# Attention and output projection: slots of one head become slots of two heads, with the parts of both heads issued kind by kind

## Chip, cores and metric

The kernel runs on one core of a Trainium2 chip. The metric is device time in microseconds of one execution, the lower the better. An execution profiled by the hardware gives the trace from which all rows below come. PE is TensorE's matmul stream, PEld its weight loads, DVE is VectorE, ACT is ScalarE, POOL is GpSimd, SP the queue that issues most transfers.

## The reference, cut to what matters

One encoder layer over two sequences of 1024 and 2048 tokens (24 blocks of 128 tokens), width 1024. After RMSNorm and one input projection, half of the width goes through a bidirectional state space model with a gated linear unit, the other half through windowed attention; both halves are normed, gated, concatenated and projected.

```python
def _attn_branch(q, k, v, sink, rel_bias):   # 8 heads of 64, 2 KV heads, blocks of 128 queries
    ...                                      # kw, vw: the block before, the block itself, the block after
    scores = jnp.einsum('bnqkgd,bnskd->bnkgqs', qb, kw)
    scores = scores * (HEAD_DIM ** -0.5) + bias
    scores = jnp.where(valid, scores, NEG_INF)            # |rel| <= 128
    m = jnp.maximum(jnp.max(scores, axis=-1, keepdims=True), sink_l)
    p = jnp.exp(scores - m)
    denom = jnp.sum(p, axis=-1, keepdims=True) + jnp.exp(sink_l - m)
    out = jnp.einsum('bnkgqs,bnskd->bnqkgd', p / denom, vw)
...
mixed = jnp.concatenate([_rmsnorm(y_ssm, ssm_norm_w) * jax.nn.silu(z_ssm),
                         _rmsnorm(y_attn, attn_norm_w) * jax.nn.silu(z_attn)], axis=-1)
return x + mixed @ w_out                                  # then a final RMSNorm
```

## The kernel before

The first part of the program (projection, state space model, gated linear unit) ends at about 896 us of the span and is not touched. What follows is the attention with the output projection: one software pipeline over the 24 blocks. A period p has eight slots h = 0 to 7, one per head, and in period p five blocks are at work: block p (scores), p-1 (transposes of the probabilities, first value product), p-2 (second value product, norm, gate), p-3 (output projection) and p-4 (final norm, store). Each engine runs its instructions strictly in the order in which the Python code issues them, so the order of calls in `attn_slot` is the order of work on PE, ACT, DVE and POOL; waits between engines come from the tiles, which are pools of a few buffers. All matrices are fp32 split into a high and a low part.

What a slot of one head issues, with the names that stand in the rows:

- `a_qk` (L1361, L1365): two matmuls into a score buffer `pssc` (two buffers, tag "sc"), then one DVE operation that adds the bias into `s` and takes the row maximum.
- `b_tr` (L1404 to L1417): two or three PE transposes of `s` into `pt` (two buffers), an ACT copy to `ph` (and `hs`, odd heads), and DVE subtractions to `pl` (and `hs`).
- `a_exp` (L1379): the exponential on ACT.
- `c_mm` (L242 to L244): two steps of the output projection, six matmuls with 512 columns into `pn`.
- once in a period: `b_pv(block p-2, second KV head)` at h = 0 and `b_pv(block p-1, first KV head)` at h = 4 (L1429): ten matmuls into `pv`, then an ACT copy (L1432) and a DVE sum (L1433) to `vlo`. The first needs `ph`, `pl` and `hs` of heads 4 to 7 of its block. `b_out` (L1442): four transposes of `vlo` into `tm`, at h = 1 and h = 5. `b_fin` at h = 2, `b_gate` (L1461, DVE) and `c_fin2` (L1527, DVE) at h = 5. `c_mix` (L1498 to L1500) at h = 6: four transposes of the gated block into `pm`, an ACT copy to `mh` and a DVE subtraction to `ml`. `c_gate` (L1482) and the second half of `c_ssm` (L1490) are POOL operations on 128x512.

The value products and the transposes of `c_mix` use the same single buffer of PSUM, by their tag:

```python
pv = pps.tile([P, 4, P], F32, tag="pv", name="pv", bufs=1)     # b_pv
pm = pps.tile([P, 4, P], F32, tag="pv", name="pm5", bufs=1)    # c_mix
```

so the next of them can start only when DVE has read the one before (L1433 or L1500). The loop advances a clock by `tick()` once per slot; stores and a few deferred steps hang on that clock.

Of the kernel before, what the change touches and what calls it, by code (L numbers as in the profile page):

```python
# [25 lines left out]
NH = 8  # L26
# [12 lines left out]
NBLK = NTOK // P  # L39
# [7 lines left out]
def f32(t):  # L47
    return t.bitcast(F32)
# [40 lines left out]
def hymba_layer_kernel(ctx, tc, x, xt, w_in, nw, lre, lim, lstep, bre, bim, cre, cim, dsk, w_glu, bglu,  # L89
# [14 lines left out]
    def load(dst, src):  # L104
        nc.sync.dma_start(out=dst, in_=src)
# [3 lines left out]
    def store(dst, src):  # L109
        store_eng[0].dma_start(out=dst, in_=src)  # L110
# [15 lines left out]
    def tick():  # L126
        now[0] += 1
        for e in [e for e in late if e[1] <= now[0]]:
            late.remove(e)
            store(e[2], e[3])  # L130
# [11 lines left out]
    def run_soon():  # L142
        for e in [e for e in soon if e[0] <= now[0]]:
            soon.remove(e)
            e[1]()
# [760 lines left out]
    for c in range(NCH):  # L906
        for ft in range(8):
# [9 lines left out]
            if c + 1 < NCH:  # L917
# [4 lines left out]
                elif ft in (1, 2) and c:  # L922
                    i = 4 * ft - 4
# [350 lines left out]
    for s in SEQS:  # L1274
        n = s // P
# [69 lines left out]
    def wo_load(k):  # L1345
        load(wor[k % 2], w_out[k * P:(k + 1) * P])

    def wo_split(k, n):
        f = slice(n * 512, (n + 1) * 512)
        split_w(*(t[:, k - 4, f] for t in wo[1]), wor[k % 2][:, f], wsc[:, k:k + 1])  # L1350
        if n and k + 2 < KM:
            wo_load(k + 2)

    pps = ctx.enter_context(pool("ps5", space=PSUM))
    def a_qk(i, h):
        d = st[i]
        pr, hf = divmod(h, 2)
        c0, nk, ko, ne, po, bo = (d["hv"][hf][k] for k in ("c0", "nk", "ko", "ne", "po", "bo"))
        ps = pps.tile([P, 384], F32, tag="sc", name="pssc", bufs=2)
        for hl in range(2):  # L1360
            TE.matmul(ps[:, 0:ne], lhsT=d["qt"][:, hf, pr * P:(pr + 1) * P],  # L1361
                      rhs=d["kt"][:, h // 4, hl, ko:ko + ne], start=hl == 0, stop=hl == 1)
        if hf == 0:
            d["sc"][pr] = p4.tile([P, 2, 320], F32, tag="s", name="s", bufs=6)
        V.tensor_tensor_reduce(out=d["sc"][pr][:, hf, c0:c0 + nk], in0=ps[:, po:po + nk], in1=bias[:, pr, bo:bo + nk],  # L1365
                               op0=ALU.add, op1=ALU.max, scale=1.0, scalar=NEG, accum_out=d["mx"][:, h:h + 1])
# [26 lines left out]
    def b_tr(i, h):  # L1393
        d = st[i]
        kv, pp, hf = h // 4, h // 2 % 2, h % 2
        v, s_ = d["hv"][hf], d["sc"][h // 2]
        if h % 4 == 0:
            for nm in ("ph", "pl"):
                d[nm, kv] = p4.tile([P, 2, 2, 2, P], F32R, tag=nm, name=nm, bufs=2)
            d["hs", kv] = p4.tile([P, 2, 2, P], F32R, tag="hs", name="hs", bufs=2)  # L1400
        pt = pps.tile([P, 3, P], F32, tag="pt", name="pt", bufs=2)
        n = len(v["full"])
        for j, (c, _) in enumerate(v["full"]):
            TE.transpose(pt[:, j], s_[:, hf, c:c + P], ident)  # L1404
        parts = [e for e in range(2) if d["hv"][e]["part"]] if hf else []
        if parts:
            m = 64 * len(parts)
            c = 256 + 64 * parts[0]
            TE.transpose(pt[0:m, 2], s_.rearrange("p f k -> p (f k)")[:, c:c + m], ident)
        hs = [(d["hs", kv][:, e, pp], pt[64 * k:64 * k + 64, 2]) for k, e in enumerate(parts)]  # L1410
        for t, p in hs:
            A.copy(out=t[0:64], in_=p)
        ph, pl = (d[nm, kv][:, hf, 0:n, pp] for nm in ("ph", "pl"))
        A.copy(out=ph, in_=pt[:, 0:n])  # L1414
        V.tensor_tensor(out=pl, in0=pt[:, 0:n], in1=f32(ph), op=ALU.subtract)  # L1415
        for t, p in hs:
            V.tensor_tensor(out=t[64:128], in0=p, in1=f32(t[0:64]), op=ALU.subtract)  # L1417
# [18 lines left out]
    def b_out(i, kv):  # L1436
        d = st[i]
        if kv == 0:
            d["tm"] = pps.tile([P, 512], F32, tag="tm", name="tm", bufs=1)
        for h in range(4):  # L1440
            hh = 4 * kv + h
            TE.transpose(d["tm"][:, hh * HD:(hh + 1) * HD], d["ot"][:, h], ident[0:64, 0:64])  # L1442
# [21 lines left out]
    def c_load(i):  # L1464
        d = st[i]
        un, bu = divmod(d["bg"], 8)
        yt = p4.tile([P, 4, P], F32, tag="ys4", name="ys4", bufs=2)
        load(yt, yssc[un][:, bu * P:(bu + 1) * P].rearrange("(k p) t -> p k t", p=P))
        zs = p4.tile([P, 4, P], F32, tag="zs4", name="zs4", bufs=2)
        load(zs, zssc[un][:, bu * P:(bu + 1) * P].rearrange("(k p) t -> p k t", p=P))  # L1470
        za = p4.tile([P, HALF], F32, tag="za", name="za", bufs=2)
        load(za, zasc[d["bg"] * P:(d["bg"] + 1) * P])
        d.update(za=za, yt=yt, zs=zs)

    def c_load_x(i):
        d = st[i]
        d["x"] = p4.tile([P, DM], F32, tag="x4", name="x4", bufs=2)
        load(d["x"], x[d["bg"] * P:(d["bg"] + 1) * P])

    def c_gate(i):  # L1480
        d = st[i]
        G.tensor_tensor(out=d["yt"], in0=d["yt"], in1=d["zs"], op=ALU.mult)  # L1482

    def c_ssm(i):
        d = st[i]
        yt = d["yt"]
        mh = p4.tile([P, 8, P], F32R, tag="mh", name="mh", bufs=2)
        ml = p4.tile([P, 8, P], F32R, tag="ml", name="ml", bufs=2)
        A.copy(out=mh[:, 0:4], in_=yt)
        G.tensor_tensor(out=ml[:, 0:4], in0=yt, in1=f32(mh[:, 0:4]), op=ALU.subtract)  # L1490
        d.update(mh=mh, ml=ml)
# [10 lines left out]
    def c_mm(i, n, k, c0=0, c1=512):  # L1502
        d = st[i]
        if k == 0 and c0 == 0:
            d["pn", n] = pps.tile([P, 512], F32, tag="pn", name="pn", bufs=2)
        f = slice(n * 512 + c0, n * 512 + c1)
        wh, wl = (t[:, k % 4, f] for t in wo[k // 4])
        mm3(d["pn", n][:, c0:c1], d["mh"][:, k], d["ml"][:, k], wh, wl, k == 0, k == KM - 1)
# [47 lines left out]
    def ok(i):  # L1556
        return 0 <= i < NBLK

    def attn_slot(p, h):
        ia, ib, it, ic, io = p, p - 1, p - 2, p - 3, p - 4  # L1560
        if ok(ia):
            a_qk(ia, h)
        if ok(it) and h == 0:
            b_pv(it, 1)
            if it:
                c_gate(it)
        if p == 0:
            if h == 5:
                c_load(0)
        elif p == 1:  # L1570
            if h == 2:
                c_gate(0)
            elif h == 5:
                c_ssm(0)
        if ok(ib):
            b_tr(ib, h)
        if h >= 4 and ok(ia):
            a_exp(ia, h - 4)
        if h < 4 and ok(ib):
            a_exp(ib, h + 4)  # L1580
        if h == 0 and ok(ic):
            c_load_x(ic)
        if p == 2:
            c_mm(0, h // 4, h % 4)
        if ic == 0:
            c_mm(ic, h // 4, 4 + h % 4)
        elif ic == NBLK - 1 and h >= 4:
            for j in range(4):
                c_mm(ic, 1, h % 2 * 4 + j, h // 6 * 256, h // 6 * 256 + 256)
        elif ok(ic):  # L1590
            for j in range(2):
                c_mm(ic, h // 4, (h % 4) * 2 + j)
        if ic == NBLK - 1:
            c_last(ic, h)
        if h == 0 and ok(io) and io < NBLK - 1:
            c_res(io, 1)
        if h == 4 and ok(ic) and ic < NBLK - 1:
            c_res(ic, 0)
        if h == 0 and ok(ib):
            a_den(ib, 0)  # L1600
        if h == 4 and ok(ib):
            a_den(ib, 1)
            b_pv(ib, 0)
        if h == 1:
            if ok(it):
                b_out(it, 1)
            if ok(io) and io < NBLK - 1:
                c_fin1(io)
        if h == 2 and ok(it):
            b_fin(it)  # L1610
            if it:
                c_ssm(it)
        if h == 3 and ok(ia):
            a_nm(ia, 0)
        if h == (4 if p else 0) and ok(ia + 1):
            a_load(ia + 1)
        if h == 5:
            if ok(ib):
                b_out(ib, 0)
            if ok(it):  # L1620
                b_gate(it)
            if ok(io) and io < NBLK - 1:
                c_fin2(io)
        if h == 6:
            if ok(it):
                c_mix(it)
            if ok(ib) and ib:
                c_load(ib)
        if h == 7 and ok(ia):
            a_nm(ia, 1)  # L1630

    wo_load(4)
    wo_load(5)
    for p in range(NBLK + 3):
        for h in range(NH):
            tick()
            attn_slot(p, h)
            run_soon()
            if p == 1:
                wo_split(4 + h // 2, h % 2)  # L1640
    flush()


# [44 lines left out]
```

## Time and profile before

| | us |
|---|---|
| median of 3 runs | 1406.27 (1405.92 to 1414.81) |
| profiled execution, its device time | 1414.28 |
| profiled execution, span from first to last instruction | 1412.5 |
| PE busy in the span | 1336.2 (95%) |
| DVE busy | 1045.4 (74%) |
| ACT busy | 745.8 (53%) |
| POOL busy | 295.0 (21%) |

The profiled execution is 8.0 us longer than the median of the three runs and within 0.6 us of the longest of them. Its device time is 1.8 us over its span. Matmuls overlap each other and their ends are modelled, so the cost of a matmul is read as the distance from its start to the start of the next one, not as its length.

### The profile page before, as it was taken

The page shows a single profiled execution, that of the slowest core. Times are in us where ns is not written, and L with a number is a line of the kernel's source. Part 1 is how long each engine was busy: PE and PEld are TensorE (multiplying, and loading weights), DVE is VectorE, ACT ScalarE, POOL GpSimd, SP SyncE. Part 2 cuts the span into 40 slices and gives each one's busy share as a digit, 9 for nine tenths or more (in the row PEclk, how much of TensorE's full clock was granted, in tenths as well). Part 3 has the DMA queues.
Part 4 walks back from the last instruction along what each step waited for, and adds up shares of the span by engine and source line. Part 5 has one row for each costly group of instructions (what it writes and reads, how often), then busy time and mean ns, then how long its engine had stood idle before and what let it go on. Part 6 is the DMA issues. An engine that isn't in the chain of part 4 may idle for free.

```text
span 1412.5 us, 24562 instructions
## 1 busy us (share of the span) xinstructions
PE 1336.2 (95%) x8578; PEld 1190.6 (84%) x8578; DVE 1045.4 (74%) x2423; ACT 745.8 (53%) x1662; POOL 295.0 (21%) x798
## 2 busy tenths in 40 slices
PE   7998999999999998999999889879999999999997
PEld 7998999999988997887797767667888888888876
DVE  5499666344897796588588378668888888888885
ACT  6222432243345525746747567566766666666662
POOL 1143231010000000000000043513444334433442
PEclk9998999999999998999999989789999999999999
DMA  7534474655556465424424564792668866766533
GB/s 255 171 122 166 169 221 148 186 168 189 172 177 200 154 195 171 156 83 154 163 90 153 173 182 151 209 215 80 145 166 195 194 173 156 178 167 162 127 98 112
DMA packets 240152, 231.22 MB, mean 164 GB/s; under 512 B 64679, under 2 KB 203187, under 8 KB 240028
## 3 DMA queue, kind: packets, MB, share of 16 engines
q1 hardware_dynamic: 215844, 197.12, 50.3%
q10 hardware_dynamic: 23784, 31.22, 6.2%
q8 instruction: 68, 1.11, 0.3%
q0 software_dynamic: 400, 1.31, 0.2%
q14 instruction: 56, 0.46, 0.1%
HBM read 156.17 MB, written 73.43 MB: 163 GB/s over the span
## 4 chain that ended last, share of the span: by engine, by line
PE 39%; DVE 14%; issue 4%; DMA 3%; ACT 3%; POOL 1%; SPq 0%; POOLq 0%; ACTq 0%; DVEq 0%
PE psv L1117 7%; PE pn L244 5%; PE pn L242 5%; PE pn L243 4%; PE pssc L1361 3%; PE pv L1429 3%; PE psc L668 2%; DVE R L642 2%; PE pt L1404 2%; DVE s L1365 1%; DVE pl L1415 1%; DMA gr<-gsc 1%; PE tm L1442 1%; PE psb L612 1%; PE psc L666 1%
## 5 line engine op out<-in xcount | busy, mean ns | idle before, releaser
L1222 POOL TENSOR_TENSOR gsa<-gsa,qt 128x512 f32<-128x512 f32 x15 | 31.7, 2112 | 553.5 <-DMA gr<-gsc 520.1
L242 PE MATMUL psj<-xhi,w1uh 128*128 128x256 f32 x384 | 113.4, 295 | 11.2 <-ACT xhi L229 7.0
L243 PE MATMUL psj<-xlo,w1uh 128*128 128x256 f32 x384 | 111.6, 291 | 0.3 <-DVE xlo L230 0.3
L244 PE MATMUL psj<-xhi,w1ul 128*128 128x256 f32 x384 | 111.2, 290 | 0.0
L1379 ACT ACTIVATE s<-s,nm 128x320 f32<-128x320 f32 (+2 forms) x192 | 106.0, 552 | 9.8 <-DVE nm L1371 9.8
L1415 DVE TENSOR_TENSOR pl<-pt,ph 128x256 fp32r<-128x256 f32 (+1 forms) x192 | 78.0, 406 | 38.5 <-ACT ph L1414 38.0
L1361 PE MATMUL pssc<-kt,qt 128*128 128x320 f32 (+1 forms) x384 | 97.4, 338 | 9.6 <-DMA qt<-qkl 5.7
L242 PE MATMUL psj<-xhi,w1zh 128*128 128x256 f32 x368 | 105.3, 286 | 0.0
L243 PE MATMUL psj<-xlo,w1zh 128*128 128x256 f32 x368 | 104.1, 283 | 0.0
L244 PE MATMUL psj<-xhi,w1zl 128*128 128x256 f32 x368 | 104.1, 283 | 0.0
L1365 DVE CUSTOM_DVE_ANT_0 s<-pssc,bias 128x320 f32<-128x320 f32 (+2 forms) x192 | 90.2, 471 | 9.9 <-PE pssc L1361 6.2
L821 ACT ACTIVATE zt<-zt 128x256 f32<-128x256 f32 x48 | 20.1, 418 | 138.6 <-DVE zt L820 132.9
L1414 ACT CAST ph<-pt 128x256 fp32r<-128x256 f32 (+1 forms) x192 | 69.4, 362 | 36.5 <-PE pt L1404 34.7
L1361 PEld LDWEIGHTS pssc<-kt,qt 128*128 128x128 f32 x384 | 67.3, 198 | 22.7 <-issue 6.1
L242 PEld LDWEIGHTS psj<-xhi,w1uh 128*128 128x128 f32 x384 | 76.7, 200 | 11.4 <-ACT xhi L229 7.0
L242 PE MATMUL pn<-wo1h,mh 128*128 128x512 f32 (+1 forms) x196 | 84.4, 431 | 0.6 <-DVE x L1513 0.6
L242 PE MATMUL pn<-wo0h,mh 128*128 128x512 f32 (+1 forms) x196 | 84.6, 431 | 0.0
L243 PEld LDWEIGHTS psj<-xlo,w1uh 128*128 128x128 f32 x384 | 76.6, 200 | 0.6 <-DVE xlo L230 0.6
L244 PE MATMUL pn<-wo0h,ml 128*128 128x512 f32 (+1 forms) x196 | 77.1, 393 | 0.0
L243 PE MATMUL pn<-wo0l,mh 128*128 128x512 f32 (+1 forms) x196 | 77.0, 393 | 0.0
L244 PE MATMUL pn<-wo1h,ml 128*128 128x512 f32 (+1 forms) x196 | 76.6, 391 | 0.0
L244 PEld LDWEIGHTS psj<-xhi,w1ul 128*128 128x128 f32 x384 | 76.5, 199 | 0.0
(485 smaller groups left out, 4448.0 us busy)
## 6 DMA issues: line engine op xcount, KB each, us to landing
xraw<-in_dram SPq DMA_DIRECT2D x44, 512.0 KB
xtok<-in_dram SPq DMA_DIRECT2D x24, 512.0 KB
x<-in_dram SPq DMA_DIRECT2D x24, 512.0 KB
out_dram<-x SPq DMA_DIRECT2D x23, 512.0 KB
xraw<-in_dram SPq DMA_DIRECT2D x11, 1024.0 KB
qkh<-qth ACTq DMA_DIRECT2D x60, 128.0 KB
qkl<-qtl SPq DMA_DIRECT2D x60, 128.0 KB
zssc<-zt ACTq DMA_DIRECT2D x48, 128.0 KB
```

What stands on the lines that cost most here:

```text
L242: TE.matmul(ps, lhsT=wh, rhs=xh, start=first, stop=False)
L243: TE.matmul(ps, lhsT=wh, rhs=xl, start=False, stop=False)
L244: TE.matmul(ps, lhsT=wl, rhs=xh, start=False, stop=last)
L642: V.tensor_tensor_scan(out=r, data0=view(d0, 0, [[1, RS]]), data1=r, initial=0.0, op0=ALU.mult, op1=ALU.add)
L1117: TE.matmul(pv[n], lhsT=xx[:, k, tk], rhs=ww[:, n * 320:(n + 1) * 320], start=s0, stop=s1)
L1222: G.tensor_tensor(out=sqs[n], in0=sqs[n], in1=sq, op=ALU.add)
L1361: TE.matmul(ps[:, 0:ne], lhsT=d["qt"][:, hf, pr * P:(pr + 1) * P], rhs=d["kt"][:, h // 4, hl, ko:ko + ne], start=hl == 0, stop=hl == 1)
L1365: V.tensor_tensor_reduce(out=d["sc"][pr][:, hf, c0:c0 + nk], in0=ps[:, po:po + nk], in1=bias[:, pr, bo:bo + nk], op0=ALU.add, op1=ALU.max, ...
L1379: A.activation(out=s_, in_=s_, func=AF.Exp, bias=d["nm"][:, h:h + 1], accum_out=d["den"][:, h:h + 1])
L1414: A.copy(out=ph, in_=pt[:, 0:n])
L1415: V.tensor_tensor(out=pl, in0=pt[:, 0:n], in1=f32(ph), op=ALU.subtract)
L1429: TE.matmul(pv[:, :, 64 * hf:64 * hf + 64], lhsT=w, rhs=r.rearrange("p a (b q) -> p (a b) q", b=2), start=e == 0, stop=e == len(ops) - 1)
```

## The change

Slots are taken two at a time (one at a time in the last period only). The body of `attn_slot` is cut into six parts: scores, value product, transposes, exponentials, output projection, and the rest. For a pair of heads each part is issued for both heads before the next part starts. So in the middle of the pipeline PE gets four score matmuls, then (first pair) the ten value matmuls, then five transposes, then twelve matmuls of the projection, and then what the rest of both heads holds. `b_out(p-1, 0)` moves from h = 5 to h = 6, ahead of `c_mix`. `tick()` is called twice ahead of each pair.

```diff
-    def attn_slot(p, h):
-        ia, ib, it, ic, io = p, p - 1, p - 2, p - 3, p - 4
-        if ok(ia):
-            a_qk(ia, h)
+    def s_scores(p, h):
+        if ok(p):
+            a_qk(p, h)
+
+    def s_values(p, h):
+        it = p - 2
         if ok(it) and h == 0:
             b_pv(it, 1)
             if it:
                 c_gate(it)
...
-        if ok(ib):
-            b_tr(ib, h)
...
+    def s_probs(p, h):
+        if ok(p - 1):
+            b_tr(p - 1, h)
+
+    def s_exp(p, h):
+        ia, ib, ic = p, p - 1, p - 3
         if h >= 4 and ok(ia):
             a_exp(ia, h - 4)
         if h < 4 and ok(ib):
             a_exp(ib, h + 4)
         if h == 0 and ok(ic):
             c_load_x(ic)
+
+    def s_mix(p, h):
+        ic = p - 3
         if p == 2:
             c_mm(0, h // 4, h % 4)
...
         elif ok(ic):
             for j in range(2):
                 c_mm(ic, h // 4, (h % 4) * 2 + j)
+
+    def s_rest(p, h):
+        ia, ib, it, ic, io = p, p - 1, p - 2, p - 3, p - 4
...
         if h == 5:
-            if ok(ib):
-                b_out(ib, 0)
             if ok(it):
                 b_gate(it)
             if ok(io) and io < NBLK - 1:
                 c_fin2(io)
         if h == 6:
+            if ok(ib):
+                b_out(ib, 0)
             if ok(it):
                 c_mix(it)
...
+    def attn_slot(p, hs):
+        for part in (s_scores, s_values, s_probs, s_exp, s_mix, s_rest):
+            for h in hs:
+                part(p, h)
+
     wo_load(4)
     wo_load(5)
     for p in range(NBLK + 3):
-        for h in range(NH):
-            tick()
-            attn_slot(p, h)
+        n = 2 if p < NBLK + 2 else 1
+        for h in range(0, NH, n):
+            for _ in range(n):
+                tick()
+            attn_slot(p, range(h, h + n))
             run_soon()
             if p == 1:
-                wo_split(4 + h // 2, h % 2)
+                for i in range(n):
+                    wo_split(4 + h // 2, i)
     flush()
```

## Rows read from the trace of the kernel before

**Rows 1.** Stretches: us, busy time by engine, granted PE clock, DMA share, GB/s.

```profile
985.00:1342.00 357.00, 352.88 (x2063) 297.91 (x2062) 303.89 (x960) 238.95 (x746) 140.68 (x450) 1.00 0.70 168
1342.00:1362.00 20.00, 19.11 (x116) 16.10 (x115) 16.87 (x54) 12.93 (x43) 7.81 (x25) 1.00 0.30 88
...
943.00:963.00 20.00, 16.08 (x93) 13.47 (x93) 15.71 (x52) 12.54 (x40) 5.23 (x14) 0.91 0.50 132
```

**Rows 2.** The chain of waits, one from 927 us, the rest 1001 to 1022 us.

```profile
927.87 0.43 PE pn L242
...
1001.38 0.44 PE pm L1498 x4
...
1011.75 0.29 PE pssc L1361 x2
1012.04 0.22 PE pt L1404 x2
...
1021.31 0.44 PE pm L1498 x4
```

**Rows 3.** Timeline at the end of one period: start, us, engine, what, [idle before <- releaser].

```profile
1097.09 0.60 PE L1498 MATMUL pm<-ident,at 128*128 128x128 f32 x4
...
1098.75 0.68 DVE L1500 TENSOR_TENSOR ml<-pm,mh 128x512 fp32r<-128x512 f32 x1
...
1099.81 0.28 PE L1429 MATMUL pv<-ph,vt 128*128 128x256 f32 x1
```

**Rows 4.** Timeline in the drain of the pipeline, period 24 to 25.

```profile
1377.23 0.63 PE L1498 MATMUL pm<-ident,at 128*128 128x128 f32 x4
...
1377.89 0.59 ACT L1499 CAST mh<-pm 128x512 fp32r<-128x512 f32 x1 [1.51 <-PE pm L1498]
...
1378.53 0.68 DVE L1500 TENSOR_TENSOR ml<-pm,mh 128x512 fp32r<-128x512 f32 x1
...
1379.27 0.19 PEld L1429 LDWEIGHTS pv<-ph,vt 128*128 128x128 f32 x1 [0.23 <-DVE ml L1500]
```

**Rows 5.** Timeline inside the second value product of one period.

```profile
1100.17 0.28 PE L1429 MATMUL pv<-pl,vt 128*128 128x256 f32 x1
1100.18 0.61 DVE L1417 TENSOR_TENSOR hs<-pt,hs 64x128 fp32r<-64x128 f32 x2
...
1100.61 0.36 PE L1429 MATMUL pv<-hs,vd 128*128 128x256 f32 x1 [0.16 <-DVE hs L1417]
```

**Rows 6.** Waits of PE and its weight loads, 985 to 1342 us: us in total, times, longest.

```profile
PE tm L1442 <- DVE vlo L1433: 2.1, 2, 1.7
PEld pv L1429 <- issue: 4.2, 14, 0.3
```

**Rows 7.** Timeline of DVE, 1092 to 1099 us.

```profile
1093.95 0.68 DVE L1433 TENSOR_TENSOR vlo<-pv,vlo 64x512 f32<-64x512 f32 x1
...
1096.02 0.75 DVE L1461 SCALAR_TENSOR_TENSOR at<-at,ra,za 128x512 f32<-128x512 f32 x1
...
1096.68 1.28 DVE L1527 SCALAR_TENSOR_TENSOR x<-x,rf,fn_sb 128x1024 f32<-128x1024 f32 x1
...
1097.99 0.49 DVE L1365 CUSTOM_DVE_ANT_0 s<-pssc,bias 128x320 f32<-128x320 f32 x1
...
1098.41 0.42 DVE L1415 TENSOR_TENSOR pl<-pt,ph 128x256 fp32r<-128x256 f32 x1
```

**Rows 8.** Timeline, POOL beside DVE in the drain of the pipeline.

```profile
1375.25 1.28 POOL L1490 TENSOR_TENSOR ml<-ys,mh 128x512 fp32r<-128x512 f32 x1
1375.46 1.62 DVE L1461 SCALAR_TENSOR_TENSOR at<-at,ra,za 128x512 f32<-128x512 f32 x1
```

**Rows 9.** Timeline of PE from a last transpose into the projection.

```profile
1095.62 0.48 PE L242 MATMUL pn<-wo1h,mh 128*128 128x512 f32 x1
...
1095.94 0.39 PE L243 MATMUL pn<-wo1l,mh 128*128 128x512 f32 x1
...
1096.16 0.40 PE L244 MATMUL pn<-wo1h,ml 128*128 128x512 f32 x1
```

More of the change, by code (lines that the diff above doesn't have):

```diff
@@ L1566, in attn_slot @@
                 c_gate(it)
[L1567 to L1574, printed above, removed]
-        if ok(ib):
-            b_tr(ib, h)
+        if p == 0 and h == 5:
+            c_load(0)
+        elif p == 1 and h == 2:
+            c_gate(0)
+        elif p == 1 and h == 5:
+            c_ssm(0)
+    def s_probs(p, h):
[3 more added lines that the diff above has]
+        ia, ib, ic = p, p - 1, p - 3
         if h >= 4 and ok(ia):
```

## The prediction

> **What bounds the kernel now.** I read first the table of stretches, then the chain of waits in one period, then the timeline around the operations that change places. From 985 to 1342 us PE is busy for 352.88 of 357 us at a granted clock of 1.00, DVE for 303.89 (85%), ACT for 67%, POOL for 39% [rows 1]. The reader is to see that this stage is PE's: whatever makes PE wait there is paid in full, and whatever shortens another engine is worth nothing unless PE waited for it. The chain of waits says the same step by step: a slot is score matmuls (0.29 us for two), transposes (0.22 for two), projection matmuls, and from one `c_mix` to the next (1001.38 to 1021.31) a period takes 19.93 us [rows 2]. DVE is the second engine, full enough that its order of work can reach PE.
>
> **The change part by part.** Nothing is added to or taken from any engine's work; only its order changes. So the sum is made of waits.
>
> Regrouping on PE: the chain charges about 0.147 us for a score, 0.11 for a transpose [rows 2], the same after one kind or another. I put the regrouping itself at nothing; the third rival prices the other reading.
>
> Order in the new period, worked out from the code. First pair: four scores, the ten matmuls of `b_pv(p-2, 1)`, five transposes, twelve projection matmuls, then `b_out(p-2, 1)`. Second pair: scores, transposes, projection. Third pair: the same, with `b_pv(p-1, 0)` at its end. Fourth pair: four scores, five transposes, twelve projection matmuls, `b_out(p-1, 0)`, `c_mix(p-2)`. And then the next period begins: four scores, `b_pv(p-1, 1)`.
>
> Added wait. `c_mix` and `b_pv` share one PSUM buffer. Before, the whole slot h = 7 and two scores lay between them: from the start of `pm` (1097.09) to the start of `pv` (1099.81) were 2.72 us, all of it PE work, and `ml`, which frees the buffer, ended at 1098.75 + 0.68 = 1099.43 [rows 3]. Its price bare is in the drain, where the trace of before has the very wait: `pm` starts at 1377.23, `mh` follows at 1377.89 for 0.59, `ml` at 1378.53 for 0.68, and the weight load of `pv` comes at 1379.27, released by `ml` [rows 4]: 2.04 us. In the new order PE has `pm` itself (0.44) and four scores (2 x 0.29 = 0.58) to do in that time [rows 2]. It then stands for 2.04 - 1.02 = 1.0 us. Queued behind the waiting value product on PE are the transposes of heads 0 and 1 and all that follows, and ACT and DVE wait for those; PE is the bound, so nothing gives it back. It comes at the border of every pair of periods from 4 to 23, 19 times: 19 x 1.0 = 19 us. In the two borders of the drain (23 to 24, 24 to 25) there are no scores any more, and the cover is `pm` alone: 2 x 1.6 = 3.2 us. Sum 22.2.
>
> Removed waits. The second value product stood for `hs` of head 7: its fourth matmul starts at 1100.17, the fifth at 1100.61, 0.44 us where about 0.12 is usual [rows 5], and the load after it comes 0.08 late: 0.4 in all. The waits list shows it in 14 of the 17 periods between 985 and 1342 us [rows 6]; two more blocks follow in which I take the same: 16 x 0.4 = 6.4. In the new order twelve projection matmuls (2.8) and four scores lie between the transposes of head 7 and that product, where six and two lay; DVE's `hs` is then early. `b_out` waited for `vlo` twice, 2.1 us [rows 6]; it now stands behind twelve projection matmuls each time, the first KV head's one slot later than before, and keeps no wait. Sum -8.5.
>
> DVE ahead of `ml`, the unknown term. In the fourth pair DVE has in its queue, from the end of `b_pv(p-1, 0)` at T: `vlo` 0.68, `b_gate` 0.75, `c_fin2` 1.28, two maxima 0.49 each, two `pl` 0.42 each [rows 7], `hs` 0.61 [rows 5]: 5.14 us, and `vlo` cannot start before ACT's copy, some 0.65 after T, so at T + 5.8 by durations; by distances of starts (`b_gate` to `c_fin2` is 0.66, not 0.75 [rows 7]) about 0.5 less, T + 5.3. PE does in the same time 0.58 of scores, 0.54 of transposes, 12 x 0.23 = 2.8 of projection, some 0.6 of `b_out`, starts `pm` at about T + 4.4, and ACT has `mh` ready 1.25 later [rows 4], at T + 5.65. So DVE comes free 0.35 early to 0.15 late. I take no added delay; bounds of the wait per border 0.9 and 1.3 us, so -2 to +6 us on the sum.
>
> The first periods. In periods 2 and 3 the projection runs at half its rate and no engine is full: from 943 to 963 us PE 16.08 of 20 us, DVE 15.71, ACT 12.54 [rows 1]. These are latencies of single heads, and two heads in flight hide a part: I estimate 1.5 of the 3.9 us idle in that stretch and as much in the one before, against two new waits of 1.0: -1, with bounds -4 and +3 (rows of the new order are not to be had from this trace). Periods 0 and 1 hang on the tail of the earlier stage and on a load; zero.
>
> Queues. SP gets the same transfers in the same order, and each is used a pair of slots or more after it is issued; POOL's order is unchanged. Put at zero; if a load came late it would be that of `c_load`, whose products POOL and then `b_gate` need, and that is the place of the second rival.
>
> Sum: 22.2 - 8.5 - 1 = **+12.7 us** on the profiled execution: 1414.28 + 12.7 = 1427. That execution lies 8.0 above the median of the three, so the median becomes 1406.27 + 12.7 = **1419 us**, 0.9% slower. A measurement of this kernel can tell about 1% from no change (14 us), so the likeliest outcome is right below what can be told.
>
> **The rivals.**
>
> 1. *The new wait does not come or is small*, while the old ones go: -8.5 - 2 (early) = -10, 1396 us. For it: the source order says nothing about how early ACT and DVE get there. Against it: the 2.04 us is a chain of three operations, each with its length in a row, and the cover of 1.02 is all that lies between [rows 4].
>
> 2. *POOL holds DVE in the fourth pair, slower.* In the drain `b_gate` started 0.21 us after a POOL operation on 128x512 and took 1.62 instead of 0.75 [rows 7, 8]. In the new order that POOL operation (second half of `c_ssm`) ends, by the lengths of the steps before it, some 0.4 us before `b_gate` may start. If it slips by half a microsecond, `b_gate` is held, `c_fin2`, both maxima, `pl`, `hs` and `ml` come up to 1.0 later, and the wait at the border is 2.0 instead of 1.0: 12.7 + 20 = +33, 1439 us. It decides from an overlap of about 0.5 us. Against it: the same margin was positive in every full period before, and each period repeats the one before it.
>
> 3. *Changing kind costs PE time, faster.* The first projection matmul after a transpose has 0.32 us to the next start, later ones 0.22 [rows 9]. Read as a price of the change, half of the eight changes per period go: 4 x 0.1 x 21 = -8. With the new wait this gives +4, 1411 us; without it -18, 1388. Against it: the record of that matmul starts 0.03 after the last transpose's, so the 0.1 us is that transpose's own time, and the chain of waits gives it to the transpose.
>
> 4. *The clock.* Between 943 and 963 us the granted clock was 0.91 with PE busy for 80%; between 1342 and 1362 it was 1.00 with PE busy for 19.11 of 20 [rows 1]. The new order leaves about 19.7 of 20.6 busy, like the second. At the lower level (1.2 GHz) a projection matmul took 0.43 us instead of 0.23 [rows 2]. If each period lost one pair of slots to it: 12 x 0.2 x 20 = +48, 1454 us. The Trainium skill, "TensorE: Matmul & The Clock Gate", Part 4, says that transposes do not count as PE being busy as other matmuls do; runs of transposes grow here from three to five. By that rule the clock could fall where transposes gather; the trace so far speaks against it, since as many transposes per period ran at a clock of 1.00.
>
> **How the numbers follow.** Forecast as worked out (+6 to +20): 0.62. Rival 1: 0.08; rival 2: 0.12; rival 3 with the wait 0.10, without it 0.05; rival 4: 0.03. Predicted time 1419. Range: the forecast's own is 1412 to 1426; taking in rival 1 and the first form of rival 3 brings the low end to 1396; rival 2 taken at four fifths, with its overlap partial, brings the high end to 1434. Outside stay the 0.05, the 0.03 and part of the 0.12. Slower by over 1% (above 1420.3): two fifths of the forecast (0.25), rival 2 and rival 4: 0.41. Faster by over 1% (below 1392.2): the second form of rival 3 and the lower edge of rival 1: 0.08. Within 1%: 0.51.
>
> **What would show it.** Right: in the changed trace the weight load of `pv` at the start of a period is released by `ml` (L1500), about 1.0 us of idle PE, 19 times, and over 1.5 twice in the drain; no wait for `hs` inside the value product; none of `b_out` for `vlo`; periods of about 20.6 us instead of 20.0 at a clock of 1.00. Wrong: periods at or under 20.0 (rival 1 or 3), `b_gate` of 1.6 us in most periods (rival 2), a clock under 1.00 after 985 us (rival 4). A prediction off by more than 10 us with the wait at 1.0 would mean that I misjudged the first periods, or that the two executions compared differ by the 8 us that already separate the runs of before.

## The result and the profile after

| | before | after |
|---|---|---|
| median of four runs, us | 1408.14 (1405.92 to 1414.81) | 1422.69 (1419.26 to 1426.66) |
| ratio | | 1.0096, 95% interval 1.0067 to 1.0125 |
| profiled execution, device time / span | 1414.28 / 1412.5 | 1419.26 / 1417.5 |

The forecast was +12.7 us (0.9% slower); the four runs give +14.6 between the medians, and the ratio is 1.0096. The two profiled executions differ by only 5.0 us, because the earlier stages, which are the same program, took 6.7 us less in the one of after. From the first score to the end of the span the two traces have 515.9 and 527.6 us: +11.7. That is the stretch that the sum was made for, and I compare it from here on.

The two tables of stretches, cut at the first score, at the score of period 4, at that of period 23 and at the end (us, busy time of PE, PEld, DVE, ACT, POOL, granted clock, DMA share, GB/s). The kernel before:

```profile
896.60:963.50 66.90, 50.51 (x250) 41.48 (x250) 49.33 (x170) 41.87 (x128) 20.26 (x49) 0.74 0.70 172
963.50:1342.00 378.50, 373.98 (x2186) 315.73 (x2186) 322.40 (x1020) 253.65 (x793) 147.20 (x474) 1.00 0.68 162
1342.00:1412.50 70.50, 60.92 (x345) 50.37 (x343) 46.63 (x131) 29.60 (x90) 23.98 (x75) 0.98 0.33 105
```

The changed kernel:

```profile
889.90:952.60 62.70, 45.89 (x250) 38.28 (x250) 49.40 (x169) 41.52 (x131) 19.89 (x49) 0.81 0.76 189
952.60:1342.70 390.10, 373.63 (x2187) 315.97 (x2186) 314.89 (x1022) 247.29 (x790) 148.31 (x475) 1.00 0.64 156
1342.70:1417.50 74.80, 62.62 (x347) 52.16 (x345) 44.36 (x130) 29.41 (x88) 23.97 (x75) 0.95 0.30 99
```

Read the PE column against the length of the stretch. In the 19 full periods PE does the same work in the same time (373.98 and 373.63 us), but stands 16.5 us instead of 4.5: the stretch is 11.6 us longer and all of it is standing. The drain is 4.3 us longer, 1.7 of it PE busy for longer at a lower clock (0.95 for 0.98). The first periods are 4.2 us shorter, and there it is PE's busy time that fell, by 4.6 us, at a higher clock (0.81 for 0.74).

The chain of waits through one period of the changed kernel (start, us, what; pieces of the projection left out), which answers to [rows 2, 4]:

```profile
1115.15 0.60 PE pm L1498 x4
1115.77 0.60 ACT mh L1499
1116.40 0.70 DVE ml L1500
1117.14 1.45 PE pv L1429 x10
1118.59 0.44 PE pt L1404 x4
...
1135.39 0.39 PE tm L1442 x4
1135.79 0.60 PE pm L1498 x4
1136.41 0.60 ACT mh L1499
1137.03 0.70 DVE ml L1500
1137.78 0.39 PE pv L1429
```

Once in a period the chain leaves PE, goes through the copy on ACT and the subtraction on DVE, and comes back: from `pm` to `pv` 1.99 us, where the drain of before had 2.04 to the weight load [rows 4]. From `pm` to `pm` it is 20.64 us, against 19.93 [rows 2].

### The profile page after: what moved, and what is told of

It is laid out like the page before. It is cut to its first block, busy times and chain, and to the rows that moved or that the text cites. A ratio compares the mean times of both kernels' runs of the same rounds, so it can differ in the third digit from the quotient of the medians.

```text
span 1417.5 us, 24568 instructions
## 1 busy us (share of the span) xinstructions
PE 1326.0 (94%) x8578; PEld 1183.3 (83%) x8578; DVE 1036.7 (73%) x2423; ACT 739.3 (52%) x1662; POOL 297.7 (21%) x798
## 4 chain that ended last, share of the span: by engine, by line
PE 46%; DVE 10%; issue 4%; ACT 3%; DMA 1%; POOL 0%; SPq 0%; POOLq 0%; ACTq 0%; DVEq 0%
PE psv L1117 7%; PE pn L242 6%; PE pn L244 6%; PE pn L243 6%; PE pv L1429 4%; PE pssc L1361 3%; PE pt L1404 3%; DVE R L642 2%; PE psc L668 2%; PE tm L1442 1%; DVE ml L1500 1%; PE psb L612 1%; PE psg L243 1%; PE psg L242 1%; PE psc L666 1%
## 5 line engine op out<-in xcount | busy, mean ns | idle before, releaser
L1365 DVE CUSTOM_DVE_ANT_0 s<-pssc,bias 128x320 f32<-128x320 f32 (+2 forms) x192 | 83.2, 468 | 9.0 <-PE pssc L1361 7.4
L1361 PE MATMUL pssc<-kt,qt 128*128 128x320 f32 (+1 forms) x384 | 78.2, 326 | 11.7 <-DMA qt<-qkl 6.7
L242 PEld LDWEIGHTS psj<-xhi,w1uh 128*128 128x128 f32 x384 | 75.9, 198 | 11.7 <-ACT xhi L229 7.2
L242 PE MATMUL pn<-wo0h,mh 128*128 128x512 f32 (+1 forms) x196 | 81.1, 414 | 0.0
L242 PE MATMUL pn<-wo1h,mh 128*128 128x512 f32 (+1 forms) x196 | 80.1, 409 | 0.6 <-DVE x L1513 0.6
L1432 ACT COPY vlo<-pv 64x512 f32<-64x512 f32 x48 | 28.0, 583 | 97.7 <-PE pv L1429 89.4
L243 PE MATMUL pn<-wo1l,mh 128*128 128x512 f32 (+1 forms) x196 | 75.7, 386 | 0.0
```

The source lines that it names most:

```text
L242: TE.matmul(ps, lhsT=wh, rhs=xh, start=first, stop=False)
L243: TE.matmul(ps, lhsT=wh, rhs=xl, start=False, stop=False)
```

## The experiments

Periods below are distances between the first scores of neighbouring blocks, worked out from the traces; interior blocks of the long sequence unless said. Before: 19.9 to 20.3 us, one of 21.7. After: 20.63 to 20.66.

**The buffer alone.** The transposes of `c_mix` take the two buffers of the probabilities' transposes instead of the one of the value products.

```diff
-        pt = pps.tile([P, 3, P], F32, tag="pt", name="pt", bufs=2)
+        pt = pps.tile([P, 4, P], F32, tag="pt", name="pt", bufs=2)
...
-        pm = pps.tile([P, 4, P], F32, tag="pv", name="pm5", bufs=1)
+        pm = pps.tile([P, 4, P], F32, tag="pt", name="pm5", bufs=2)
```

> The changed kernel, with the transposes of c_mix in the two buffers of the probabilities' transposes (tag pt) instead of the value products' one (tag pv); same order, same instructions. Theory (the shared buffer makes PE stand 1.1 us at the start of each period, and the regrouping itself costs and gives nothing): the wait of pv for ml is gone, periods 20.66 - 1.1 = 19.6 us, 19 of them, two longer waits in the drain (3.4 us) and the clock lost after them gone too, so 25 to 29 us under the changed kernel, 12 to 15 under the kernel before (ratio 0.990). Rival (PE is slower in the new order for another reason, and waits at pv only because it is there anyway; DVE comes late): the wait moves to hs or to the next transposes, periods stay above 20.2, within 5 us of the changed kernel.

Measured: 1401.87 us, 0.9938 of the kernel before (0.9915 to 0.9961), 20.8 under the median of the changed kernel. Periods 19.73 to 19.75, no wait of `pv` for `ml`; the full periods fall from 390.1 to 371.9 us. The gain fell 4 us short of what was expected; 0.2 us a period are left in a wait of `pm` for `pl`. The timeline of the border (compare with the chain above: `pv` now starts before `ml`, 1.07 us after `pm`):

```profile
1095.35 0.42 PEld L1498 LDWEIGHTS pm<-ident,at 128*128 128x128 f32 x4 [0.27 <-DVE pl L1415]
1095.36 0.66 PE L1498 MATMUL pm<-ident,at 128*128 128x128 f32 x4
...
1096.43 0.28 PE L1429 MATMUL pv<-ph,vt 128*128 128x256 f32 x1
...
1096.67 0.69 DVE L1500 TENSOR_TENSOR ml<-pm,mh 128x512 fp32r<-128x512 f32 x1 [0.41 <-ACT mh L1499]
```

**The wait alone, in the old order.** Slots of one head; only `c_mix` moves to the end of h = 7.

```diff
-            if ok(it):
-                c_mix(it)
...
         if h == 7 and ok(ia):
             a_nm(ia, 1)
+        if h == 7 and ok(it):
+            c_mix(it)
```

> The kernel before, slots of one head, with c_mix alone moved from h = 6 to the end of h = 7, so that pv of the next period follows it after two scores. Theory (the wait follows from the order of pm and pv alone): 2.04 - 0.44 - 0.29 = 1.3 us of wait for ml per border, the 0.4 us wait for hs inside pv hidden behind it, so +0.9 x 20 and two waits of 1.6 in the drain: +18 to +24 us, 1427 to 1432. Rival (the wait needs the paired order, DVE's and ACT's queues above all): less than +8 us.

Measured: 1436.02 us, 1.0186 (1.0162 to 1.0210), periods 21.0 to 21.7. The list of waits from 985 to 1362 us has it under the name that was forecast:

```profile
PE pv L1429 <- DVE ml L1500: 21.6, 18, 1.4
```

So the order of `pm` and `pv` makes the wait in either grouping; the cost was some 2 us over the range given.

**More cover, and DVE's queue.** In the changed kernel `c_mix` goes between the projections of heads 6 and 7.

```diff
         elif ok(ic):
             for j in range(2):
                 c_mm(ic, h // 4, (h % 4) * 2 + j)
+        if h == 6 and ok(p - 2):
+            c_mix(p - 2)
...
-            if ok(it):
-                c_mix(it)
```

> The changed kernel, with c_mix issued between the projection matmuls of heads 6 and 7, so that six matmuls (1.4 us), four transposes and four scores lie between pm and pv in place of four scores. Theory with DVE's queue (hs of head 7 stands ahead of ml on DVE and ended 0.23 us before ml could start in the changed kernel): the wait only shrinks from 1.1 to 0.8 or 0.9 us, -4 to -7 us against the changed kernel. Rival (the wait is cover against the 2.04 us chain alone): the wait goes wholly, -21 us or more.

Measured: 1416.47 us, 1.0043 (1.0023 to 1.0063), 6.2 under the changed kernel; periods 20.43. Six projection matmuls and the four transposes of `b_out` as further cover took off 0.23 us a period and no more. ACT had `mh` ready at 1137.29, but DVE's timeline shows `ml` 1.55 us later, back to back behind `hs`, which stands behind `c_fin2`, two maxima and two `pl`:

```profile
1134.78 0.73 DVE L1461 SCALAR_TENSOR_TENSOR at<-at,ra,za 128x512 f32<-128x512 f32 x1
1135.44 1.27 DVE L1527 SCALAR_TENSOR_TENSOR x<-x,rf,fn_sb 128x1024 f32<-128x1024 f32 x1
1136.64 0.48 DVE L1365 CUSTOM_DVE_ANT_0 s<-pssc,bias 128x320 f32<-128x320 f32 x1
...
1137.46 0.74 DVE L1415 TENSOR_TENSOR pl<-pt,ph 128x256 fp32r<-128x256 f32 x2
1138.21 0.59 DVE L1417 TENSOR_TENSOR hs<-pt,hs 64x128 fp32r<-64x128 f32 x2
1138.84 0.69 DVE L1500 TENSOR_TENSOR ml<-pm,mh 128x512 fp32r<-128x512 f32 x1
```

Then the same with `c_fin2` moved behind `ml`:

```diff
             if ok(it):
                 b_gate(it)
-            if ok(io) and io < NBLK - 1:
-                c_fin2(io)
...
         if h == 7 and ok(ia):
             a_nm(ia, 1)
+        if h == 7 and ok(io) and io < NBLK - 1:
+            c_fin2(io)
```

> The pairs with c_mix between the projections of heads 6 and 7, and c_fin2 (1.28 us on DVE) moved from h = 5 to the end of h = 7, behind ml. Theory (there ml waited only for DVE's queue, where it followed hs back to back): ml comes up to 1.28 us earlier, the wait of pv (0.85) goes wholly, periods 20.43 to 19.6, -15 to -18 us against that run. Rival (ACT's queue holds mh as long): the wait keeps 0.5 us or more.

Measured: 1410.10 us, 1.0003 (0.9986 to 1.0020). The periods did fall to 19.6 (19.59 to 19.64, three of 20.0) and the wait of `pv` went. The total gained 6.4 us where 15 to 18 were expected: the full periods as a whole gave 10.2 (384.1 to 373.9; besides the three of 20.0, the period from block 4 to block 5 took 21.77), and the first periods took 1.8 us, the drain 0.8 us and the earlier stages 1.6 us more than in the run before it.

**Both.** `pm` in the buffers of `pt`, and `c_fin2` late (the two diffs above together).

> The pairs with pm in the buffers of pt, and c_fin2 moved behind ml to the end of h = 7. Theory: what is left there of waiting is 0.2 us of pm for pl of head 6 on DVE; it goes, periods 19.73 to 19.55, 3 to 4 us under that run, about 0.991 of the kernel before. Rival (the 0.2 us is a price of the change from transposes of 64 rows to 128 rows): periods stay at 19.7.

Measured: 1401.18 us, 0.9933 (0.9913 to 0.9954): the best of this study, though no more than 0.7 us under the first experiment, which the intervals cannot tell apart. Periods 19.54, one of 20.23: the wait of `pm` for `pl` went as expected. The stretch that answers to [rows 1], from 985 to 1342 us; PE stands 0.5 us in 357 where it stood 4.1 before:

```profile
985.00:1342.00 357.00, 356.52 (x2111) 304.71 (x2110) 302.46 (x988) 239.15 (x769) 149.38 (x468) 1.00 0.68 172
```

**The shared buffer in the old order.** The first diff, applied to the kernel before.

> The kernel before, slots of one head, with pm in the buffers of pt alone. Theory (in the old order a slot covered the reading of pm, so that the shared buffer cost nothing): periods stay 20.0, within 3 us of the kernel before. Rival (the shared buffer costs in either order, and freeing it is what gains): periods 19.6 or less, -8 us or more.

Measured: 1419.27 us, 1.0070 (1.0051 to 1.0089), periods 20.5 to 20.9: both expectations missed, on the slow side. Nine tiles a period now go through two buffers, and with slots of one head the transposes wait for DVE's `pl` of the slot before (985 to 1362 us):

```profile
PE pt L1404 <- DVE pl L1415: 12.2, 16, 0.9
```

So freeing the value products' buffer is not a gain by itself; it is the cure of what the paired order brought, and the paired order gives it room.

**The old wait for `hs`.** Slots of one head, the second value product behind the projection of h = 0.

```diff
         if ok(it) and h == 0:
-            b_pv(it, 1)
             if it:
                 c_gate(it)
...
+        if ok(it) and h == 0:
+            b_pv(it, 1)
         if ic == NBLK - 1:
```

> The kernel before, slots of one head, with b_pv(p-2, 1) alone moved behind the projection matmuls of h = 0. Theory: the wait of 0.4 us for hs of head 7 inside the product goes in some 16 periods, -5 to -7 us, periods 19.6 to 19.7, the same as the paired order without its wait: grouping by kind gives PE nothing. Rival (half the changes of kind save 0.4 us a period): periods here stay above those of the paired order without wait by 0.4 us.

Measured: 1446.55 us, 1.0242 (1.0213 to 1.0271). The wait for `hs` did go, and another one came: `tm` for `vlo`, 22.4 us in 15 waits of up to 1.8. I took it for the distance between the product and its transposes, and moved `b_out` too.

```diff
         if h == 1:
-            if ok(it):
-                b_out(it, 1)
...
         if h == 2 and ok(it):
+            b_out(it, 1)
             b_fin(it)
```

> As the run with the late value product in slots of one head, and b_out(p-2, 1) moved with it, from h = 1 to h = 2 ahead of b_fin, so that a slot lies between the product and the transposes of its result. Theory (that run lost 36 us because the transposes of the result came one slot after the product and stood 1.9 us for vlo): that wait goes and the wait for hs stays away, periods 19.6, 5 to 8 us under the kernel before. Rival (moving the product holds up DVE or the buffer of c_mix): periods above 20.3.

Measured: 1443.21 us, 1.0253 (1.0228 to 1.0278). Nothing gained, so that account was wrong: it is the other product's `vlo`, at h = 4. Its timeline:

```profile
1164.49 0.58 ACT L1432 COPY vlo<-pv 64x512 f32<-64x512 f32 x1
...
1165.09 1.30 POOL L1490 TENSOR_TENSOR ml<-ys,mh 128x512 fp32r<-128x512 f32 x1
...
1165.42 0.99 DVE L1387 TENSOR_TENSOR den<-den,se 128x4 f32<-128x4 f32 x1
...
1166.44 0.68 DVE L1391 RECIPROCAL dn<-den 64x2 f32<-64x2 f32 x4
1167.15 0.68 DVE L1433 TENSOR_TENSOR vlo<-pv,vlo 64x512 f32<-64x512 f32 x1
1167.89 0.33 PEld L1442 LDWEIGHTS tm<-ident,vlo 64*128 64x128 f32 x4 [1.95 <-DVE vlo L1433]
1167.89 0.46 PE L1442 MATMUL tm<-ident,vlo 64*128 64x64 f32 x4 [1.52 <-DVE vlo L1433]
```

ACT's copy is done at 1165.07, but DVE has `den` and its four reciprocals ahead of `vlo`. `den`, four numbers per partition, takes 0.99 us instead of 0.15 because a POOL operation on 128x512 has just begun, and `vlo` starts 2.1 us after the copy. The later `b_fin` had moved POOL's operation into `den`'s way. This is the second rival's mechanism at another place. The kernel before has it there once: `den` at 1314.4 us took 1.15 us beside the same POOL operation, `tm` then stood 1.66 us for `vlo`, and that period is the one of 21.7. I tried it by issuing `den` behind the product.

```diff
-            a_den(ib, 1)
             b_pv(ib, 0)
+            a_den(ib, 1)
```

> As the run with the value product late and b_out at h = 2, and a_den(p-1, 1) issued behind b_pv(p-1, 0) at h = 4, so that DVE does vlo ahead of den. Theory (there POOL's subtraction on 128x512, shifted by the later b_fin, held den for 0.83 us in 17 of 20 periods, vlo came late behind it, PE stood 1.5 us at tm and then ran 3.4 us at half clock): the wait at tm and the low clock go, periods fall from 21.3 to 22.9 to 19.6, 5 to 8 us under the kernel before. Rival (vlo is late for another reason, ACT's copy or the buffer): periods stay above 21.

Measured: 1423.24 us, 1.0094 (1.0071 to 1.0116). The wait at `tm` and the low clock went, 20 us with them; but not the rest: `pm` now waits for the gated block (`at`), 12.0 us in 19 waits, probably because the later `b_fin` also makes `b_gate` late (not tested). The last attempt was a smaller move, the product behind the two transposes of h = 0, ahead of the projection.

```diff
         if ok(it) and h == 0:
-            b_pv(it, 1)
             if it:
                 c_gate(it)
...
         if ok(ib):
             b_tr(ib, h)
+        if ok(it) and h == 0:
+            b_pv(it, 1)
```

> The kernel before, slots of one head, with b_pv(p-2, 1) moved behind the two transposes of h = 0 only (0.22 us later), ahead of the projection, all else in place. Theory: the wait for hs shrinks from 0.3 to 0.1 us and POOL's order in time does not change, so -0.2 to -0.3 us in 16 periods, 3 to 5 us under the kernel before, periods 19.75. Rival (any delay of that product pushes the transposes of its result into a wait for vlo): +10 us or more.

Measured: 1402.89 us, 0.9948 (0.9931 to 0.9965): 6.4 us less from the first score to the end (509.5), 3.1 of them in the full periods, the rest in the first periods and the drain. Inside one such product the fifth matmul came 0.19 us after the fourth, for 0.44 before [rows 5]. But the forecast for the periods missed: most of the 3.1 us is the one period of 21.7, which did not come here, and the ten periods from block 11 to block 21 take 200.8 us, for 200.7 before. There the matmuls of the product gave back 1.0 us and the steps from the projection to `tm` took 2.0 more, in waits for `vlo`. So no run in slots of one head isolates the price of the wait for `hs`: each time another wait took its place.

**The drain.** The changed kernel with slots of one head from period 23 on.

```diff
-        n = 2 if p < NBLK + 2 else 1
+        n = 2 if p < NBLK - 1 else 1
```

> The changed kernel with slots of one head from period 23 on. Theory: one border (22 to 23) keeps a wait of 1.3 us, the two of 1.7 us in the drain go and with them the stretch of 3.4 us at the lower clock behind the first; the stretch from period 23 to the end falls from 74.8 to 71 us, 3 to 5 us under the changed kernel. Rival (the drain is longer because of the paired order itself): it stays at 74 or more.

Measured: 1421.20 us, 1.0080 (1.0055 to 1.0104); the stretch from period 23 to the end 70.7 us, for 70.5 in the kernel before, full periods unchanged (390.1 us). Its total is 1.5 us under the changed kernel's median, less than the 4.1 us that the stretch lost, and within the spread of the earlier stages. The stretch that had the low clock, in the changed kernel, and here the stretches around the same place, which this execution reaches 5.8 us later:

```profile
1365.00:1368.00 3.00, 3.00 (x16) 2.83 (x15) 0.79 (x2) 1.38 (x5) 1.27 (x1) 0.58 0.97 320
```

```profile
1368.00:1371.00 3.00, 2.81 (x19) 2.41 (x18) 2.42 (x9) 1.48 (x7) 0.00 (x0) 1.00 0.90 276
1371.00:1380.00 9.00, 9.00 (x50) 7.19 (x49) 6.21 (x17) 6.52 (x22) 5.09 (x18) 1.00 0.34 114
```

## Why the prediction was right

**The added wait: right.** The list of who waited for `pm`'s readers in the changed kernel, over all 23 borders:

```profile
PEld pv L1429: 27.4, 23
PE pv L1429: 21.6, 23
```

21.6 us of standing PE, for which I had 24.2: 22.2 in 21 borders, and 2.0 in the first two, counted with the first periods. In the full periods (952.6 to 1342.7 us) it is 16.5 us in 19 waits by PE, 21.2 by the weight loads. From the start of `pm` to that of `pv` are 2.06 us there, and 1.07 in the run with the other buffer, whose order is the same: 1.0 a period. In the drain `pm` started at 1362.63 and the weight load of `pv` at 1364.68: 2.05 us with nothing but `pm` between them. The experiment on the buffer and the one in the old order show that it is this wait and that it needs neither pairs nor kinds.

**The removed waits: right in kind.** No wait of `pv` for `hs` and none of `tm` for `vlo` by PE stands in the list of after from 985 to 1362 us. In the full periods the net is +11.6 us (378.5 to 390.1), worked out from +19.0 and, for the share of the removed waits in these periods, -7.7 (14 x 0.4 + 2.1): +11.3. That the two agree to 0.3 us is partly luck. By distances of starts the added waits cost 21.8 us (1.15 a border with the matmul behind each, taken against the run with the other buffer, and inside the bounds of 0.9 to 1.3), the removed ones gave 8.8 (5.8 for `hs`, 3.0 for `vlo`), and the order of kinds 1.5. Of what `vlo` gave, 1.7 us is the single wait behind the `den` held at 1314.4 us in the trace of before, and no cost of every period.

**DVE ahead of `ml`: right, and by little.** I had DVE free between 0.35 early and 0.15 late (PE's terms add up to T + 4.5, not 4.4, which makes it 0.5 early to even). In the changed kernel it stood 0.23 us before `ml`:

```profile
1137.03 0.69 DVE L1500 TENSOR_TENSOR ml<-pm,mh 128x512 fp32r<-128x512 f32 x1 [0.23 <-ACT mh L1499]
```

Only at the first two borders was DVE late: `ml` began 0.73 us after `mh` was ready, and PE stood 1.4 us each time instead of the 1.0 that I had. With `c_mix` moved ahead, DVE's queue became the limit at once, and moving `c_fin2` behind took that away: the margin was real and thin.

**The regrouping itself: next to nothing, as taken.** Rival 3, which asked for -8 us, is out. By distances of starts over the 19 full periods, the scores took 2.1 us less in the changed kernel: the first score of a group costs 0.03 us more than the next, which "the same after one kind or another" had overlooked, and there are half as many groups. The transposes of `b_out` and `c_mix` took 1.1 us more, the projection with the transposes ahead of it 0.4 less: -1.5 us in all. The best paired order comes to 19.54 a period, against 20.07 before in the ten periods from block 11: the difference is about 0.3 for `hs`, 0.1 for `vlo` and 0.1 for the scores.

**The first periods: sign right, reason wrong.** I had -1 from latencies hidden by two heads in flight. The two traces differ by -4.2, and the tables of stretches put it on PE's busy time (50.51 to 45.89) at a clock of 0.81 instead of 0.74; standing time is the same (16.4 and 16.8). The run with the changed drain has the same order in these periods and repeats the figures (63.0 us at a clock of 0.81). Other paired orders had 64.6 to 66.4 us, orders with slots of one head 65.0 to 67.2, at clocks of 0.74 to 0.82 in no fixed relation to the order; how much the order itself does for the clock there stays open.

**The drain: the mechanism right, one part missed.** The stretch from period 23 holds three of the borders counted (1.0 and 2 x 1.6) and two old waits of 0.4: forecast +3.4, measured +4.3, of which 2.6 is standing and 1.7 PE busy for longer. The latter is rival 4, in one place: behind the first of the two long waits, which ended at 1364.68, the granted clock from 1365 to 1368 was 0.58 (rows above), and a projection matmul took 0.43 us to the next start instead of 0.23. I had looked at the clock for the repeated waits of 1.0 us, where it held, and not for the two longer ones. Cut into the same three stretches, the forecast was -2.0 (the wait at the border 3 to 4 falls into the full periods), +11.3 and +3.4, and the measurement is -4.2, +11.6 and +4.3: the total is as near as it is because the misses in the first periods and in the drain have opposite signs.

**The other rivals.** Rival 1 (no wait) is out. Rival 2 did not come in the changed kernel (`at` 0.73 us at the median; one of 24, in the first periods, reached 1.73, and before two in the drain took 1.62 [rows 8] and 1.42), but its mechanism was met in the runs with the later product. It was also at work in the kernel before, which the prediction did not see: 19 of 48 `den` took 0.45 to 1.24 us there beside POOL, and none over 0.18 in the changed kernel. In the full periods that is 8.3 us of DVE's time, and it accounts for the fall of DVE's busy time from 322.40 to 314.89. Rival 4's 1454 us left out the 12.7 of the forecast, and the chances for "slower by over 1%" add up to 0.40, not 0.41. Of rival 4's rule from the Trainium skill, that transposes do not count as PE being busy as other matmuls do ("TensorE: Matmul & The Clock Gate", Part 4), the trace shows no effect: with runs of five transposes the granted clock from 952.6 to 1342.7 us was 1.00.

## What to carry to other kernels

When work is regrouped on an engine that is already full, list for each shared buffer what lies between its last reader and its next writer in the new order, and price the chain of readers against that; here a pair of operations that had a slot between them came 1.0 us too close, and that ate what the regrouping removed. A cure can be a move to another tag whose buffers have room in the new order, but the same move in the old order cost 0.7%. Moving one step on one engine moves the operations of others that hang on it, and these can collide with a third: after each such move read the waits again, not only the one that was meant.

## What the runs showed of the hardware

DVE operations with two tensors in SBUF that came while POOL worked on 128x512 lasted until POOL was done and longer: `den` took 0.99 instead of 0.15 us in the timeline above, `at` 1.62 instead of 0.75 [rows 7, 8]. All 19 held `den` of the kernel before ended 0.01 to 0.02 us behind POOL's operation, both held `at` 0.55 us behind it. Others were not held: `vlo` and `pl`, which read PSUM, kept their 0.68 and 0.41 us beside POOL, and so did the reciprocals of `dn` (one small tensor in SBUF, 0.16 us).

Single waits of PE can cost more than their length. The granted clock fell to its lower level behind one of the two long waits in the drain of the changed kernel, not behind the other, and behind some of those at `tm` (1.5 us) in the run with the later product and `b_out`, where periods of 21.3 and 22.9 us alternate irregularly. It stayed at 1.00 through the 19 waits in the full periods of the changed kernel (one of 1.4 us, the others up to 0.9) and through those of up to 1.4 us in the old order with the late `c_mix`. In the run with the later product and `b_out`, the stretches before, with and behind one wait:

```profile
1160.00:1165.00 5.00, 5.00 (x31) 4.44 (x31) 3.07 (x12) 4.10 (x13) 3.58 (x17) 1.00 1.20 212
1165.00:1169.00 4.00, 2.48 (x15) 1.79 (x15) 3.87 (x12) 1.52 (x6) 1.39 (x2) 1.00 0.49 125
1169.00:1172.00 3.00, 3.00 (x12) 2.42 (x11) 2.94 (x6) 0.92 (x3) 0.00 (x0) 0.57 0.00 0
```

Identical earlier stages took between 889.9 and 897.8 us from one profiled execution to the next; effects of a few us in this kernel are read from the stretch that changed, not from the total.
